# A residual stream kept by tokens instead of by features in a two-layer transformer trunk

## The chip, the cores and the metric

The kernel runs on one core of one Trainium2 chip. The metric is the device time of one execution in microseconds (us), the median of several runs. A profile of one execution stands beside it, with the busy time of each engine: PE (TensorE, the matrix products), PEld (the loading of the standing operand into TensorE, which overlaps PE), DVE (VectorE), ACT (ScalarE), POOL (GpSimd) and SP (SyncE, which here only issues DMAs).

## What is computed

The reference is a trunk of two macaron layers on 512 tokens of 1024 features, in float32:

```python
D_MODEL, SEQ, DEPTH, D_FF, NORM_EPS = 1024, 512, 2, 2816, 1e-6

def rms_norm(x, gain):
    inv = lax.rsqrt(jnp.mean(x * x, axis=-1, keepdims=True) + NORM_EPS)
    return x * inv * gain

def swiglu(h, w_gate, w_up, w_down):
    return (jax.nn.silu(h @ w_gate) * (h @ w_up)) @ w_down

for l in range(DEPTH):
    x = x + 0.5 * swiglu(rms_norm(x, ffn1_norm[l]), ffn1_wg[l], ffn1_wu[l], ffn1_wd[l])
    z = rms_norm(x, mix_norm[l]) @ w_in[l]            # q | k | v | conv_B | conv_C | conv_h
    attn = sliding_window_attention(q, k, v, sink[l])  # window 128, 8 heads of 64, 2 for k and v
    conv = B * depthwise_causal_conv3(C * h)
    x = x + concat([attn, conv]) @ w_out[l]
    x = x + 0.5 * swiglu(rms_norm(x, ffn2_norm[l]), ffn2_wg[l], ffn2_wu[l], ffn2_wd[l])
return rms_norm(x, final_norm)
```

The root in a norm is a sum over the 1024 features of one token, so it is one number for each token. The gain is one number for each feature.

## The kernel before

**Numbers as pairs.** Every operand of a product is cut into a rounded high part and a low part that holds the rest. Each product is then three: high by high, high by low, low by high, summed in PSUM. A weight tile (128 partitions x 1024 numbers, 512 KB) is loaded by SP, its high part is cast on ACT (`split`, L200), and DVE subtracts to get the low part (L201). In the "far" form (`split_far`, L203 to L207) ACT writes the negated raw tile as the low part, casts the high part after it, and a DMA that POOL issues adds the raw tile onto the low part; DVE isn't used.

**Fewer products.** Large products are done in a scheme with seven block products in place of eight (`CHAINS`, `FORMS`, `SHARES`). The activations are cut into four blocks, two halves of the features by two halves of the tokens (called b11, b21, b12, b22 and their sums t1 to t4, made by `Seven.make`), and the weights too (a11, a12, a22 and their sums s1 to s4). One step takes one of the operands with one form of the weights, and the accumulators x, w and y are read after each step. The sums of weight blocks are partly made by DVE in the raw tiles themselves: `need_split` adds s1 into the raw a11 tile in place (L222) when it comes to the form s2.

**One order for the weights.** `plan` (L320) writes down, before anything runs, the order in which weight tiles are needed. `take_split` hands out the next pair and asks for the split of the tile two places ahead (`SPLIT_AHEAD`), and `need_raw` asks for loads four units further ahead (`LOAD_AHEAD`). There are eight raw buffers and three each of the high and the low part. Each engine takes its instructions in the order of the program, so what is issued first goes first on that engine, whether or not PE needs it first.

**Layout.** Before, the residual x lies by features: `xs[c]` holds 128 features on the partitions and 512 tokens along the row. A product into x therefore has the weight standing in TensorE and the activations moving past it. In a full plain product 512 tokens move past (`group` L269, `level`, `down` L292 to L318). In a seven step that goes into x it is `stand` (L733, product at L740): half of the tokens at a time, rows of 256. The other form, `stream` (L749, product at L755), has the activations standing, 128 tokens at a time, and 512 columns of weights moving past; it gives its result by tokens. It serves the gate and up products of the fast blocks, whose results are then turned by TensorE transposes (L961), and the last FFN.

**Stages of one FFN.** An FFN is a list of stages: `p` is a plain block of 256 hidden features, `w` two such blocks in seven steps with `stream` (`winograd2`), `u` one block in seven steps with standing weights and rows of 256 (`winograd`), `d` the plain product into x for the blocks named, and `s` the product into x for four blocks in seven steps (`share`, L764). Three of the four FFNs use `INNER` or `LAST` (p of block 0, d of block 0, five `w`, two `s`, d of blocks 9 and 10), the first uses `FIRST`. The mix has its own body (`mix`, L1194) and ends with a share into x.

**Norms.** `Norm` (L406) works by features. As soon as a stretch of x is final, `take` or `take_half` multiplies it by the gain and splits it; no root is in it yet. Squares are summed over the feature tiles, and a product with a matrix of ones (`factors`) gives the sum over the partitions, hence `inv`, one number for each token in every partition. The first products of the next stage (block 0 of an FFN; k, v and the first q in a mix) run on the unscaled x, and their results are multiplied by `inv` on the way out of PSUM. `scale` then makes the fully scaled activations for the seven steps of the later blocks. In the mixes all projections run on unscaled x, and DVE and POOL multiply by `inv` afterwards. At the end `Finale` turns x to tokens by 32 transposes, in the first steps of a `w` stage.

The function that holds all this is `trunk_kernel`; the main loop is at L1405.

Of the kernel before, what the change touches and what calls it, by code (L numbers as in the profile page):

```python
# [39 lines left out]
LAST = INNER[:-1] + (("d", (9, 10)),)  # L40
# [16 lines left out]
)  # L57


@with_exitstack  # L60
def trunk_kernel(
# [49 lines left out]
    def form(name, dt=F32R, shape=(P, KC // 2, H)):  # L111
        return xpool.tile(list(shape), dt, tag="xf", bufs=14, name=name)
# [19 lines left out]
    NROW = 16 + 2 * 16 + 24  # L132
    rows = [work.tile([n, P], F32, tag=f"rows{n}", bufs=1, name=f"rows{n}") for n in (16, NROW - 16)]
    sink = const.tile([P, DEPTH * NH], F32, name="sink")

    def load_rest():
        for i, w in enumerate((mix_norm, ffn2_norm)):
            nc.sync.dma_start(
                rows[1][16 * i : 16 * i + 16, :], w.rearrange("l (c p) -> (l c) p", p=P)
            )  # L140
        nc.sync.dma_start(rows[1][32:56, :], conv_w.rearrange("l k (c p) -> (l k c) p", p=P))
        nc.sync.dma_start(sink, attn_sink.rearrange("l h -> (l h)").partition_broadcast(P))
# [10 lines left out]
    def turn_rows(i):  # L153
        n = rows[i].shape[0]
        rp = psum("aux", [P, n], f"par_ps{i}")
        nc.tensor.transpose(rp, rows[i], ident[:n, :n])
        nc.scalar.copy(par[:, 16 * i : 16 * i + n], rp)

    def gain_of(i, c):

        at = 16 * (i % 3) + 8 * (i // 3) + c
        return par[:, at : at + 1]

    def conv_of(l, k, c):
        at = 48 + 12 * l + 4 * k + c
        return par[:, at : at + 1]
# [121 lines left out]
    def abreast(kc):  # L288

        return max(1, KC // kc) if kc in (2, 4) else 1  # L290

    def level(n, hi, lo, rhs, wide):  # L292

        accs = [psum("mm", [P, S], f"acc_{n}_{j}") for j in range(wide)]
        cols = [slice(j * P, (j + 1) * P) for j in range(wide)]
        for k, (xh, xl) in enumerate(rhs):
            for j in range(wide):
                nc.tensor.matmul(accs[j], hi[:, k, cols[j]], xh, start=k == 0, stop=False)
                nc.tensor.matmul(accs[j], lo[:, k, cols[j]], xh, start=False, stop=False)
            for j in range(wide):  # L300
                nc.tensor.matmul(
                    accs[j], hi[:, k, cols[j]], xl, start=False, stop=k + 1 == len(rhs)
                )
        return accs

    def down(rhs, fresh=False):

        wide = abreast(len(rhs))
        for c in range(0, KC, wide):
            n, hi, lo = take_split()  # L310
            if fresh and c == 0:
                yield from enumerate(level(n, hi, lo, rhs, wide))
                continue
            for j in range(wide):
                cols = slice(j * P, (j + 1) * P)
                own = (f"{n}_{j}", hi[:, :, cols], lo[:, :, cols])
                tag = ("sc", "sc", "aux", "aux")[j] if fresh else "mm"
                yield c + j, group(rhs, own=own, tag=tag)  # L318

    def plan():  # L320
        def cols(src, k0, kc, n, how=None):
            wide = abreast(kc)
            for b in range(0, n, wide):
                order.append((add_unit((src, k0, kc, b * P, wide * P)), how))

# [15 lines left out]
        def seven(at, how):  # L341
# [6 lines left out]
            order.extend((u, (what, h, how(what, h))) for what in FORMS for h in range(2))  # L348

        def ffn(wg, wu, wd, stages):  # L350
            for what, b in stages:
                how = "far" if b == (0,) and stages is not FIRST else None
# [16 lines left out]
                if stages is not LAST or b[-1] < FF // (2 * P) - 1:  # L369
                    cols(wd, 2 * b[0], 2 * len(b), KC, how)  # L370
                    continue
                for half in range(2):
                    for k in range(0, 2 * len(b), 2):
                        u = add_unit((wd, 2 * b[0] + k, 2, half * S, S))
                        if half == 0:
# [18 lines left out]
    xpair = [xpool.tile([P, 2, S], F32, tag=f"x{c}", name=f"x{c}") for c in range(KC // 2)]  # L394
    xs = [xpair[c // 2][:, c % 2, :] for c in range(KC)]
# [10 lines left out]
    class Norm:  # L406
        def __init__(self, i):
            self.i = i
            self.h = [None] * KC
            self.acc = None  # L410
            self.inv = None
            self.pairs = {}
            self.begun = set()
            self.order = range(KC)

        def take(self, c, src=None):

            xc = xs[c] if src is None else src
            g = gain_of(self.i, c)
            if c % 2 == 0:  # L420
                self.pair = [form(f"x{n}_{self.i}_{c}", shape=(P, 2, S)) for n in "hl"]
            hi, lo = (t[:, c % 2, :] for t in self.pair)
            self.h[c] = (hi, lo)
            nc.scalar.activation(hi, xc, AF.Copy, scale=g)
            nc.vector.scalar_tensor_tensor(lo, xc, g, f32(hi), op0=ALU.mult, op1=ALU.subtract)

        def square(self, c):
            if self.acc is None:
                self.acc = work.tile([P, S], F32, tag="nacc", bufs=1, name=f"nacc_{self.i}")
                nc.scalar.activation(self.acc, xs[c], AF.Square)  # L430
                return
            sq = work.tile([P, S], F32, tag="nsq", bufs=2, name=f"nsq_{self.i}_{c}")
            nc.scalar.activation(sq, xs[c], AF.Square)
            nc.vector.tensor_add(self.acc, self.acc, sq)

        def take_half(self, o, t):


            self.order = (4, 5, 6, 7, 0, 1, 2, 3)
            at = slice(t * H, (t + 1) * H)  # L440
            for m in range(2 * o, 2 * o + 2):
                if m not in self.pairs:
                    self.pairs[m] = [form(f"x{n}_{self.i}_{m}", shape=(P, 2, S)) for n in "hl"]
                for j in range(2):
                    c = 2 * m + j
                    g = gain_of(self.i, c)
                    hi, lo = (p[:, j, at] for p in self.pairs[m])
                    self.h[c] = tuple(p[:, j, :] for p in self.pairs[m])
                    nc.scalar.activation(hi, xs[c][:, at], AF.Copy, scale=g)
                    nc.vector.scalar_tensor_tensor(  # L450
# [993 lines left out]
```

## Time and profile before

| | us |
|---|---|
| median of 3 runs | 1683.12 |
| lowest, highest run | 1682.5, 1683.18 |
| span of the profiled execution | 1681.6 |
| first product of PE after the start of the span | 1.19 |

The span reaches from the first to the last instruction that the profiler saw in one execution; the time of a run has a little more around it, 1.5 us between this span and the median. The page of the profile has numbered parts: busy time by engine; the span in 40 slices, each digit a busy share in tenths, with the clock that TensorE was granted; DMA queues; the chain of work that ended last; and the costliest groups of instructions. In such a group the line of the program comes first, then engine, operation, result <- operands, partitions x elements and the count; behind the bar stand the busy time, the mean of one in ns, and the idle time ahead of it with what ended it. Matmuls are pipelined, so the duration of one is longer than the distance to the next.

### The profile page before, as it was taken

The page shows a single profiled execution, that of the slowest core. Times are in us where ns is not written, and L with a number is a line of the kernel's source. Part 1 is how long each engine was busy: PE and PEld are TensorE (multiplying, and loading weights), DVE is VectorE, ACT ScalarE, POOL GpSimd, SP SyncE. Part 2 cuts the span into 40 slices and gives each one's busy share as a digit, 9 for nine tenths or more (in the row PEclk, how much of TensorE's full clock was granted, in tenths as well). Part 3 has the DMA queues.
Part 4 walks back from the last instruction along what each step waited for, and adds up shares of the span by engine and source line. Part 5 has one row for each costly group of instructions (what it writes and reads, how often), then busy time and mean ns, then how long its engine had stood idle before and what let it go on. Part 6 is the DMA issues. An engine that isn't in the chain of part 4 may idle for free.

```text
span 1681.6 us, 23537 instructions
## 1 busy us (share of the span) xinstructions
PE 1672.6 (99%) x9010; PEld 1444.0 (86%) x9010; DVE 1381.3 (82%) x1820; ACT 964.9 (57%) x1335; POOL 206.3 (12%) x185
## 2 busy tenths in 40 slices
PE   9999999999999999999999999999999999999998
PEld 7888889988898888889988888999888988888886
DVE  7987679988899877799798777997688997667995
ACT  6445565466566655564465555654565766555654
POOL 0011111001211111111011111110012111111111
PEclk9999999999999999999999999999999999999999
DMA  8467777731497777788567777784125867777881
GB/s 251 99 177 190 186 198 184 189 94 51 119 233 163 183 181 187 187 197 203 164 138 181 191 185 183 189 230 143 51 63 140 225 138 201 187 178 185 226 211 51
DMA packets 191590, 283.14 MB, mean 168 GB/s; under 512 B 9004, under 2 KB 77684, under 8 KB 191476
## 3 DMA queue, kind: packets, MB, share of 16 engines
q1 hardware_dynamic: 151572, 200.73, 37.8%
q0 software_dynamic: 39184, 80.23, 28.0%
q8 instruction: 71, 1.16, 0.3%
q10 hardware_dynamic: 720, 0.66, 0.1%
q14 instruction: 43, 0.35, 0.1%
HBM read 261.14 MB, written 2.10 MB: 157 GB/s over the span
## 4 chain that ended last, share of the span: by engine, by line
PE 97%; DVE 2%; DMA 0%; issue 0%; ACT 0%; SPq 0%; DVEq 0%; ACTq 0%
PE x L755 25%; PE y L755 12%; PE x_s L740 8%; PE acc L279 8%; PE acc L280 8%; PE acc L282 7%; PE w L755 6%; PE y_s L740 4%; PE x_s L755 3%; PE w_s L740 2%; PE at L961 2%; PE x_m L740 1%; PE y_m L740 1%; PE y_s L755 1%; PE acc L635 1%; PE pt L1291 1%
## 5 line engine op out<-in xcount | busy, mean ns | idle before, releaser
L200 ACT CAST wh<-raw 128x1024 fp32r<-128x1024 f32 (+1 forms) x486 | 507.5, 1045 | 546.5 <-PE x L755 129.1
L201 DVE TENSOR_TENSOR wl<-raw,wh 128x1024 fp32r<-128x1024 f32 (+1 forms) x486 | 589.2, 1215 | 203.6 <-ACT wh L200 202.2
L279 PE MATMUL acc<-xh,wh 128*128 128x512 f32 x424 | 166.5, 393 | 0.0
L280 PE MATMUL acc<-xl,wh 128*128 128x512 f32 x424 | 165.6, 391 | 0.0
L282 PE MATMUL acc<-xh,wl 128*128 128x512 f32 x416 | 162.3, 390 | 0.0
L195 POOL DMA_DIRECT2D raw<-in_ffn_wu_dram x39 | 48.9, 1254 | 416.9 <-DMA raw<-in_ffn_wu_dram 338.1
L280 PEld LDWEIGHTS acc<-xl,wh 128*128 128x128 f32 x424 | 79.7, 188 | 16.3 <-DVE xl L450 0.6
L279 PEld LDWEIGHTS acc<-xh,wh 128*128 128x128 f32 x424 | 79.8, 188 | 15.7
L282 PEld LDWEIGHTS acc<-xh,wl 128*128 128x128 f32 x416 | 78.1, 188 | 16.3
L195 POOL DMA_DIRECT2D raw<-in_ffn_wg_dram x39 | 47.6, 1243 | 223.6 <-DMA raw<-in_ffn_wu_dram 89.2
L227 DVE TENSOR_TENSOR raw<-raw,raw 128x1024 f32<-128x1024 f32 x58 | 70.3, 1219 | 3.8 <-DMA raw<-in_ffn_wu_dram 2.1
L195 POOL DMA_DIRECT2D raw<-in_ffn_wd_dram x32 | 38.6, 1205 | 260.6 <-DMA raw<-in_ffn_wd_dram 159.1
L755 PE MATMUL w<-wh,fb21h 128*128 128x512 f32 x152 | 60.7, 399 | 0.0
L755 PE MATMUL x<-wh,ft2h 128*128 128x512 f32 x152 | 60.6, 398 | 0.0
L755 PE MATMUL y<-wh,ft3h 128*128 128x512 f32 x152 | 60.4, 398 | 0.0
L755 PE MATMUL w<-wl,fb21h 128*128 128x512 f32 x152 | 59.4, 391 | 0.0
L755 PE MATMUL x<-wl,ft2h 128*128 128x512 f32 x152 | 59.3, 390 | 0.0
L755 PE MATMUL y<-wh,ft3l 128*128 128x512 f32 x152 | 59.2, 390 | 0.0
L755 PE MATMUL y<-wl,ft3h 128*128 128x512 f32 x152 | 59.2, 390 | 0.0
L755 PE MATMUL w<-wh,fb21l 128*128 128x512 f32 x152 | 59.2, 389 | 0.0
L755 PE MATMUL x<-wl,fb11h 128*128 128x512 f32 x152 | 59.2, 389 | 0.0
L755 PE MATMUL x<-wl,ft1h 128*128 128x512 f32 x152 | 59.2, 389 | 0.0
(504 smaller groups left out, 4814.6 us busy)
## 6 DMA issues: line engine op xcount, KB each, us to landing
raw<-in_ffn_wu_dram SPq DMA_DIRECT2D x126, 512.0 KB, 4.4
raw<-in_ffn_wd_dram SPq DMA_DIRECT2D x104, 512.0 KB, 5.0
raw<-in_ffn_wg_dram SPq DMA_DIRECT2D x86, 512.0 KB, 4.7
raw<-in_ffn_wu_dram POOLq DMA_DIRECT2D x39, 512.0 KB, 8.1
raw<-in_ffn_wg_dram POOLq DMA_DIRECT2D x39, 512.0 KB, 6.1
raw<-in_w_in_dram SPq DMA_DIRECT2D x36, 512.0 KB, 3.7
raw<-in_ffn_wd_dram POOLq DMA_DIRECT2D x32, 512.0 KB, 8.6
raw<-raw POOLq DMA_DIRECT2D x20, 512.0 KB, 6.8
```

The costliest lines, as they stand in the source:

```text
L195: nc.gpsimd.dma_start(out=r, in_=rows_of(*more), accum_op=ALU.add)
L200: nc.scalar.copy(hi, raw)
L201: eng.tensor_sub(lo, raw, f32(hi))
L227: nc.vector.tensor_add(a11, a11, s1)
L279: nc.tensor.matmul(acc, hi[:, k, :], rhs[k][0], start=k == first, stop=False)
L280: nc.tensor.matmul(acc, hi[:, k, :], rhs[k][1], start=False, stop=False)
L282: nc.tensor.matmul(acc, lo[:, k, :], rhs[k][0], start=False, stop=k == last)
L635: nc.tensor.matmul(opening[n], (lo if part == "w" else hi)[:, k, :], xl if part == "x" else xh, start=n not in begun, stop=k == KC - 1 and ...
L740: nc.tensor.matmul(accs[c // 2][:, c % 2, :], w[:, k, cols], x_[:, 2 * h + k, :], start=start and c % 2 == 0 and h + k + i == 0, stop=h + ...
L755: nc.tensor.matmul(accs[u], x_[:, 2 * h + k, tok], w[:, k, :], start=start and h + k + i == 0, stop=h + k == 2 and i == 2, skip_group_chec ...
L961: nc.tensor.transpose(tp[:, t * P : (t + 1) * P], ups[t][:, c * P : (c + 1) * P], ident)
L1291: nc.tensor.transpose(tp[:, h, :], self.p[:, h, kb * P : (kb + 1) * P], ident)
```

## The change

x is kept by tokens through the whole program: `xt(t, o)` is a tile of 128 tokens by 512 features, four token tiles and two feature halves, in the same memory as before.

- Every product into x now has the activations standing and 512 columns of weights moving past them. `stand` and `level` are gone; `share` always uses `stream`, and `down` works on four token accumulators for each half of the features.
- `Norm` is new. As each tile of x becomes final, ACT squares it and sums along the row. When the four tiles of a token half are there, `stage` makes the root of two token tiles on ACT and four small DVE operations, and `turn` multiplies each tile by the root and by the gain (loaded by `begin` as a row spread over all partitions, two DMAs of 256 KB on SP), transposes it in four 128 x 128 pieces on TensorE, and copies the result by ACT into the activations of the next stage. For a mix it is split into high and low parts by ACT and DVE instead. So the first products of the next stage take x already scaled.
- The order of the last three steps of a share is changed (`CHAINS2`, `SHARES`), so that the first token half is final after step 4 and the second after steps 5 and 6 (`ENDS`).
- `INNER` and `LAST` begin with `w` of block 0 and end the hidden blocks with `u` of block 10; block 8 joins the plain product at the end. The far form of the first weight moves with it, from block 1 to block 0.
- A mix opens k, v and the first q together, by token halves, with rows of 256; the multiplications by `inv` are gone.
- The first norm of the program keeps the old way, in a class `First`. `Finale` no longer needs its 32 transposes.

```diff
 INNER = (
-    ("p", 0), ("d", (0,)), ("w", 1), ("w", 3), ("w", 5), ("w", 7), ("w", 9), ("s", 1), ("s", 5),
-    ("d", (9, 10)),
+    ("w", 0), ("w", 2), ("w", 4), ("w", 6), ("w", 8), ("u", 10), ("s", 0), ("s", 4),
+    ("d", (8, 9, 10)),
 )
...
-SHARES = ((0, 0, 1), (0, 0, 1), (1, 0, -1), (1, 1, 1), (1, 1, -1), (1, 0, 1), (0, 1, 1))
+SHARES = ((0, 0, 1), (0, 0, 1), (1, 0, -1), (1, 1, 1), (1, 0, 1), (1, 1, -1), (0, 1, 1))
+ENDS = {1: (0, 0), 4: (1, 0), 5: (1, 1), 6: (0, 1)}
...
+CHAINS2 = CHAINS[:4] + (CHAINS[5], CHAINS[4], CHAINS[6])
...
+    def down(acts, blocks):
+
+        for o in range(2):
+            accs = [psum("mm", [P, S], f"down_{state['group']}_{t}") for t in range(NT)]
+            for i, b in enumerate(blocks):
+                _, wh, wl = take_split()
+                ah, al = acts[b]
+                for t in range(NT):
+                    tok = slice(t * P, (t + 1) * P)
+                    for k in range(2):
+                        for n, (a, w) in enumerate(((ah, wh), (al, wh), (ah, wl))):
+                            nc.tensor.matmul(
+                                accs[t],
+                                a[:, k, tok],
+                                w[:, k, :],
...
+                    if i + 1 == len(blocks):
+                        yield t, o, accs[t]
...
-                        lambda what, h: "far" if (b, what, h) == (1, "a11", 0) else None,
+                        lambda what, h: "far" if (b, what, h) == (0, "a11", 0) else None,
...
+        def begin(self):
+
+            self.gain = [g2(f"gain_{self.i}_{o}") for o in range(2)]
+            for o in range(2):
+                nc.sync.dma_start(
+                    self.gain[o], self.row[o * S : (o + 1) * S].partition_broadcast(P)
                 )
...
+        def __call__(self, t, o):
+
+            nc.scalar.activation(
+                junk(f"sq_{self.i}_{t}_{o}"),
+                xt(t, o),
+                AF.Square,
+                accum_out=self.ss[:, o * NT + t : o * NT + t + 1],
+            )
+            half = t // 2
+            self.seen[half] += 1
+            if self.seen[half] == 4:
+                self.stage(half)
+
+        def stage(self, half):
+
+            i = self.i
+            if half == 0:
+                self.rooms()
+            v, r, y = (small(f"{n}_{i}_{half}", 2) for n in "vry")
+            at = 2 * half
+            nc.vector.tensor_add(v, self.ss[:, at : at + 2], self.ss[:, NT + at : NT + at + 2])
+            nc.scalar.activation(r, v, AF.Abs_reciprocal_sqrt, scale=1.0 / D, bias=eps)
+            nc.vector.tensor_scalar(v, v, 1.0 / D, EPS, op0=ALU.mult, op1=ALU.add)
+            newton(y, r, v)
+            for o in range(2):
+                for t in (at, at + 1):
+                    self.turn(t, o, y[:, t - at : t - at + 1])
+                if half == 0 and not self.mixing:
+                    self.make(("b11", "b21")[o])
+            if half and not self.mixing:
+                self.make("t2")
+
+        def turn(self, t, o, by):
+
+            name = f"{self.i}_{t}_{o}"
+            tok = slice(t * P, (t + 1) * P)
+            xn = g2(f"xn_{name}")
+            nc.vector.scalar_tensor_tensor(
+                xn, xt(t, o), by, self.gain[o], op0=ALU.mult, op1=ALU.mult
+            )
+            tp = psum(self.tags.pop(0), [P, KC // 2, P], f"xt_{name}")
+            for j in range(KC // 2):
+                nc.tensor.transpose(tp[:, j, :], xn[:, j * P : (j + 1) * P], ident)
+            if self.mixing:
+                hi, lo = (p[:, :, tok] for p in self.parts[o])
+                nc.scalar.copy(hi, tp)
+                nc.vector.tensor_sub(lo, tp, f32(hi))
+            else:
+                nc.scalar.copy(self.full[o][:, :, tok], tp)
...
-        for step, (acc, operand, start) in enumerate(CHAINS):
+        for step, (acc, operand, start) in enumerate(CHAINS2):
...
-                if y is None:
-                    stand(accs[acc], wh, wl, xh, xl, h, start)
-                else:
-                    stream(accs[acc], wh, wl, xh, xl, h, start)
+                stream(accs[acc], wh, wl, xh, xl, h, start)
...
-                    if y is None:
-                        part = xpair[2 * o + m][:, :, t * H : (t + 1) * H]
-                    else:
-                        part = y[2 * t + m][o]
+                    part = xt(2 * t + m, o)
                     nc.vector.scalar_tensor_tensor(
                         part, accs[acc][m], by * sign, part, op0=ALU.mult, op1=ALU.add
                     )
+                    if after and step in ENDS:
+                        after(2 * t + m, o)
...
-        kacc, vacc, qacc = norm.groups(3)
...
+        held = [take_split(SPLIT_AHEAD - j) for j in range(3)]
+        kacc, vacc, qacc = opened = [psum("mm", [P, S], f"acc_{n}") for n, _, _ in held]
+        for t in range(2):
+            tok = slice(t * H, (t + 1) * H)
+            for j, (_, hi, lo) in enumerate(held):
+                for k in range(KC):
+                    xh, xl = (z[:, tok] for z in norm.h[k])
...
-        share(ops, 1.0, after.step, soon={(0, 1): ("t2",), (1, 0): ("t1",), (1, 1): ("t3", "t4")})
+        after.begin()
+        share(ops, 1.0, soon={(0, 1): ("t2",), (1, 0): ("t1",), (1, 1): ("t3", "t4")}, after=after)
```

More of the change, by code (lines that the diff above doesn't have):

```diff
@@ L286, in group @@
         return acc
[L288 to L318, printed above, removed]
+    def down(acts, blocks):
[12 more added lines that the diff above has]
+                                w[:, k, :],
+                                start=i + k + n == 0,
+                                stop=i + 1 == len(blocks) and k == 1 and n == 2,
+                            )
+                    if i + 1 == len(blocks):
+                        yield t, o, accs[t]
@@ L347, in seven @@
                     add_unit(*(at(o, j, h) for o, j in what))
-            order.extend((u, (what, h, how(what, h))) for what in FORMS for h in range(2))
+            order.extend((u, (what, h, how(what, h))) for what in forms for h in range(2))
         def ffn(wg, wu, wd, stages):
             for what, b in stages:
-                how = "far" if b == (0,) and stages is not FIRST else None
                 if what == "p":
@@ L526, in make @@
                     continue
-                hi, lo = (form(f"f{what}{n}_{self.name}") for n in "hl")
+                hi, lo = both(f"f{what}_{self.name}")
                 self.forms[what] = (hi, lo)
@@ L553, in room_form @@
     def room_form(name):
-        return [form(f"sum{n}_{name}", F32) for n in range(2)]
-    norm = Norm(0)
+        return both(f"sums_{name}", F32)
+    norm = First()
     s8 = small("s8", 2 * NT)
@@ L950, in winograd2 @@
                 turns(step)
-                if not first and step < 3:
-                    norm.make(CHAINS[step + 4][1])
+                if not first and step < 4:
+                    norm.make(("t3", "t1", "t4", "b22")[step])
                 if between:
```

386 lines of the change are left out of this document (145 added, 241 removed).

## Prediction

> **What bounds the kernel now.** I read the page first (busy shares, clock row, chain of work that ended last), then the list of who waited for whom on PE, then the merged chain in order of time for the pace of each kind of product.
>
> ```profile
> span 1681.6 us, 23537 instructions
> ...
> PE 1672.6 (99%) x9010; PEld 1444.0 (86%) x9010; DVE 1381.3 (82%) x1820; ACT 964.9 (57%) x1335; POOL 206.3 (12%) x185
> ...
> PEclk9999999999999999999999999999999999999999
> ...
> PE 97%; DVE 2%; DMA 0%; issue 0%; ACT 0%; SPq 0%; DVEq 0%; ACTq 0%
> ```
>
> ```profile
> PE idle L127 <- DVE warm L582: 1.2, 1, 1.2
> PE y_m L740 <- DVE wl L201: 0.5, 2, 0.3
> PE xt L601 <- DMA xin<-in_x_dram: 0.2, 1, 0.2
> ```
>
> PE is the bound from one end to the other: it stands still for 1.9 us in all, 97% of the chain is PE, and the clock is full after the first slice. DVE at 82% is next. So the time follows PE's own work plus whatever makes PE wait; any wait that the change opens is paid in full, because nothing else is on the chain.
>
> PE's work must be counted by pace, not by the duration of one product, since products overlap:
>
> ```profile
> 150.26 10.88 PE x L755 x48
> ...
> 740.58 5.75 PE x_s L740 x48
> 746.34 5.76 PE w_s L740 x48
> ```
>
> ```profile
> 172.82 0.38 PE L961 MATMUL at<-ident,u 128*128 128x128 f32 x2
> 173.04 0.38 PE L961 MATMUL at<-ident,p 128*128 128x128 f32 x2
> 173.25 0.38 PE L961 MATMUL at<-ident,u 128*128 128x128 f32 x2
> 173.47 0.38 PE L961 MATMUL at<-ident,p 128*128 128x128 f32 x2
> 173.61 0.47 PE L755 MATMUL y<-wh,ft3h 128*128 128x512 f32 x1
> ```
>
> A 512 wide product takes 10.88/48 = 0.2267 us, a 256 wide one 5.76/48 = 0.120, a 128 wide transpose (173.25 - 172.82)/4 = 0.108. So two products of 256 cost 0.240 where one of 512 costs 0.227.
>
> **The change: PE's own work.** Counts are from the code and from the instruction order of the two built programs.
>
> - Eight shares (two each in the three fast FFNs that end in `x<-`, one each in the two mixes) go from `stand` to `stream`: 336 products of 256 (40.3 us) become 168 of 512 (38.1), 2.23 each, -17.9.
> - In three FFNs `p` of block 0 (96 of 512, 21.8 us) becomes `u` of block 10 (168 of 256, 20.2): -4.8. The plain down products stay at 144 per FFN.
> - Norm sums by the ones matrix: ten products of 512 go, -2.3.
> - The mixes open with 144 products of 256 by token halves for 72 of 512: 2 x 0.96, +1.9.
> - Transposes: five norms x 32 come, the 32 at the end go: 128 x 0.108, +13.8. The longer end (block 8 joins it, block 0's down goes): +0.1.
>
> Sum -9.2 us; in all 5512 + 2976 + 520 products (512, 256, 128 wide) become 6408 + 1092 + 648.
>
> **DVE, ACT, DMA.** The programs hold 1741 DVE instructions for 1820, 1248 on ACT for 1244, 409 SP transfers for 398 (ten broadcasts of gains, issued one stage ahead, are hidden behind that stage), POOL loses its ten multiplications by `inv`. Totals are no bound. A share at 38.1 instead of 40.3 us could be, as its DVE work is nearly as long. The last FFN already has such a share:
>
> ```profile
> 1566.00:1607.00 41.00, 41.00 (x183) 33.95 (x182) 40.79 (x44) 23.69 (x24) 6.58 (x6) 1.00 0.90 234
> ```
>
> There PE runs 183 products in 41 us without a gap while DVE is at 40.79 of 41. So 0 is the near row; the far end is 1 us for each of four first shares, +4. I take 0.
>
> **The change: what now waits.** Before, the first products of a stage take x unscaled, and `inv` comes in behind them; a norm is off PE's path. After, x must be squared, rooted, scaled, transposed, copied and split before the stage's first product. Half of the tokens is turned ahead, the second half must fit behind two operands' products. Rows for this chain:
>
> ```profile
> L201 DVE TENSOR_TENSOR wl<-raw,wh 128x1024 fp32r<-128x1024 f32 x479 | 585.0, 1224 | 198.1 <-ACT wh L200 196.7
> ...
> L791 DVE SCALAR_TENSOR_TENSOR x<-x_s,x 128x512 f32<-128x512 f32 x48 | 31.8, 684 | 0.8
> ...
> L1156 DVE SCALAR_TENSOR_TENSOR ytok<-ytok,y_end,gain 128x512 f32<-128x512 f32 x3 | 2.2, 746 | 0.0
> ...
> L402 DVE TENSOR_TENSOR y_end<-r_end 128x1 f32<-128x1 f32 x4 | 0.6, 160 | 0.4 <-ACT r_end L1121 0.3
> ```
>
> ```profile
> L200 ACT CAST wh<-raw 128x1024 fp32r<-128x1024 f32 x479 | 503.7, 1052 | 544.8 <-PE x L755 129.1 <-issue 89.8 <-PE y L755 84.3
> L965 ACT COPY raw_a<-at 128x512 f32<-128x512 f32 x64 | 35.8, 586 | 3.1 <-PE at L961 3.0
> ...
> L496 ACT ACT_TABLE_LOAD x5 | 6.4, 1283 | 0.1
> ...
> L1115 ACT ACTIVATE ysq<-ytok 128x512 f32<-128x512 f32 x5 | 3.1, 629 | 6.1 <-DVE ytok L1113 6.0
> ...
> L1115 ACT ACTIVATION_READ_ACCUMULATOR ysq<-ytok 128x1 f32 x7 | 1.3, 186 | 0.0
> ...
> L695 ACT ACTIVATE r<-v,eps 128x4 f32<-128x4 f32 x1 | 0.3, 298 | 0.0
> ```
>
> ```profile
> L207 POOL DMA_DIRECT2D wl<-raw x9: 856/896/896, 523.1 to 1363.8; - x9
> ...
> DMA to landing us min/median/max: 4.4/7.5/8.9
> ```
>
> I walk each engine's queue in the order of the built program. Back to back, DVE operations follow each other about 0.08 us sooner than their durations say.
>
> *Mix to FFN (twice).* Zero is where PE ends step 4 of `share`, the last into token half 0, second column half. ACT: weight cast to 1.1, two squares to 2.7, table load to 4.0, root to 4.3. DVE: x update and three small operations to 5.4, a weight's low part to 6.6, four scaled tiles at 7.3 to 9.3. PE: step 5 to 5.4, then step 6 with the first transposes in it (0.35 lost) to 13.0. ACT meanwhile copies and casts b11 to 10.3, b21 to 13.1. DVE ends b11's low part at 11.5, and now stands the new wait: next in its queue is the add into the raw weight (L222), and that weight is the source of the "far" copy whose ACT part ended at 7.1 and which lands 7.5 later, 14.65. Queued behind it are both last x updates, b21's low part and the second half's scaling; ACT's squares and through them the cast of the b21 weight wait for them. So: add 15.8, x 16.4, b21 low 17.6, weight low 18.7, x 19.3, weight low 20.5, then (add, root, three small, add) 23.4 and scaled tiles 24.2 to 26.2. PE's queue has b21's products first: weight cast ready 18.4, four products, low part 20.5, eight products to 22.35; the next b21 weight lies in the buffer just read, cast 22.4 to 23.45, four products; transposes as the tiles come; streaming from 26.75. From 12.97 that is 13.8 us with 18 products and 16 transposes in it (5.8): idle 7.9 + 0.35 = 8.3. With a landing of 4.4 it is 5.2, with 8.9 it is 9.7.
>
> *FFN to FFN (once).* Zero is the start of the last down unit, 5.44 us long; its last two quarters are the other token half, so the first half has only 2.7 us of cover. The far copy leaves at -3.3 and lands at 4.2; the add into its source stands ahead of the first x update of the unit. DVE: add 5.4, weight low 6.6, x 7.2 and 7.8, add 8.9; ACT: squares 9.0, table 10.3, root 10.6; scaled tiles 11.9 to 13.9; first transpose 11.95, so PE stands 6.5 us. Then, as above, b11, b21, second root, second tiles 20.4 to 22.4, and PE streams from 22.9: 17.4 us after 5.44, work in it 5.5, idle 11.9 (8.8 to 13.0 by the landing).
>
> *FFN to mix (once).* No far copy. Squares of three quarters 5.8, table 7.1, root 7.4, tiles from 8.7; second tiles 16.2 to 18.2; PE streams at 18.7: 13.3 us less 8.3 of work, idle 5.0. *First FFN's share to mix (once)*: same chain with steps 5 and 6 as cover, idle 2.3 (0.3 + 0.7 + 1.3 at three places).
>
> Idle together 2 x 8.3 + 11.9 + 5.0 + 2.3 = 35.8, from 26.5 to 39.7 by the landing alone. If the cover were whole, 0.
>
> **The clock.** A long pause may cost more than itself:
>
> ```profile
> 1.19 2.74 PE L127 MATMUL idle<-zero 128*128 128x512 bf16 x6 [1.19 <-DVE warm L582]
> ...
> 4.91 1.49 PE L601 MATMUL xt<-ident,xin 128*128 128x128 f32 x6
> ...
> 8.20 0.60 PE L601 MATMUL xt<-ident,xin 128*128 128x128 f32 x4
> ```
>
> The same transposes come 0.21 apart at 4.9 us and 0.11 apart at 8.2: PE starts at half pace and keeps it for about 5.0 us from its first product. [...] From the rows, a fall costs 0 to half of 5.0 us, 2.5, per pause: 0 to 7.5. I take 2.5: only the FFN to FFN pause (6.5) is longer than the 5.0 us that the start shows.
>
> **Sum**, against the profiled execution: 1681.6 - 9.2 + 35.8 + 2.5 = 1710.7; the median of the runs, 1683.12, lies 1.5 above the span: 1712.
>
> **Rivals.**
> 1. *The cover is whole, and the change is faster.* If the second half's chain, from the last product into x to its last split, ends within the 10.9 us of products on b11 and b21, and PE finds those first in its queue ready, only PE's own work is left: 1683.1 - 9.2 = 1674. It decides at 2.7 us of first-half cover after an FFN and at 10.9 us after a share. For it: ACT is idle 43% of the time. Against it: by the rows the first half alone takes 6.5 us too long, and the built order puts b21 ahead of b11 and its raw add ahead of the x updates.
> 2. *Part of the waits is hidden*: far copies land at 4.4 and half of the rest overlaps, about 13 us idle: 1681.6 - 9.2 + 13 + 1.5 = 1687, up to 1699 where only the landing is early.
> 3. *The clock falls in every pause*: 1712 + 5 = 1717; with late landings (39.7) 1721.
> 4. *DVE becomes the bound in the faster shares*: +4, 1716, by the row above not likely.
> 5. *The change doesn't do what it says* (512 wide products slower with x standing): the row at 150.26 is that very form, so no.
>
> **How the numbers follow.** Forecast with waits about as walked (1699 to 1717, rival 4 within it): 0.60. Rival 3: 0.13. Rival 2: 0.17, a quarter of it within 0.2%. Rival 1: 0.10. The range leaves out rival 1 and the low part of rival 2 at one end and the last of rival 3 at the other: 1690 to 1722. A difference of 0.2% (3.4 us) is about what a measurement of this kernel can tell from none. Faster 0.10, same 0.05, slower 0.85.
>
> **What would show it.** In the page after: PE busy under 99%, idle of about 36 us, nearly all of it at five places, ahead of the first products on b21 and the norm transposes, put down to DVE (scaled tiles, weight low parts) and ACT (casts); DVE waiting for the far copy at the raw add three times; products of 512 at 0.227, shares of 38.1 us. If PE's pauses are absent the walk is wrong; if they are there but the time is 5 us higher with products 0.45 apart behind them, it is the clock; if PE waits inside shares, it is DVE.

## The result, and the profile after

The changed kernel takes **1748.2 us** (median of 4 runs, 1744.71 to 1752.14), the kernel before 1683.14 beside it: a ratio of 1.0388, 95% interval 1.0373 to 1.0403. The forecast was 1712, with a range up to 1722. The sign was right, the size was not: 65 us slower instead of 29.

The page of the changed kernel, its busy times and the granted clock:

```profile
span 1747.0 us, 21808 instructions
...
PE 1691.9 (97%) x8150; PEld 1408.2 (81%) x8150; DVE 1334.4 (76%) x1741; ACT 966.9 (55%) x1379; POOL 194.6 (11%) x175
...
PEclk9999999999998999999989999999999999999999
```

PE's busy time went up by 19 us although its work went down. Products at half speed account for some 11.8 us of that (9.2 and 2.6 in the table below), and two slices of the clock fell; the rest of the rise was not split. Who waited for whom on PE, longest first (columns: total us, times, longest):

```profile
PE w L742 <- ACT wh L195: 10.8, 4, 5.6
PE x_s L742 <- ACT wh L195: 8.0, 6, 2.6
PE xt L512 <- DVE xn L507: 7.5, 3, 3.9
PE y_m L742 <- DVE x L771: 4.5, 2, 2.5
PE x_s L742 <- DVE x L771: 3.6, 6, 0.8
PE y_s L742 <- ACT wh L195: 2.7, 3, 0.9
PE w L742 <- ACT fb L195: 2.1, 1, 2.1
...
PE y_s L742 <- DVE x L771: 1.1, 4, 0.6
```

Rows with `xt`, `w` are at the norms, as forecast. Rows with `x_s`, `y_s`, `y_m` are inside the shares, where the forecast had nothing. In the kernel before, all waits of PE together were 1.9 us.

To place the loss, PE's **lost time** is counted from the trace: the distance from the start of each product to the start of the next, less the pace of its kind (0.2267, 0.120 or 0.108 us). It holds the pauses and the extra time of products at half speed. Before, it was 10.2 us in all; after, 84.9. Span less lost time is PE's own work, with about 8 us ahead of the first product and behind the start of the last, which are the same in both: 1671.4 us before and 1662.1 after, 9.3 less. Each column is one profiled execution. In us, with the extra time of products at half speed that no pause follows in brackets:

| place | forecast | after | old order | and late splits | and no far copy | and no root |
|---|---|---|---|---|---|---|
| first FFN to mix | 2.3 | 2.1 | 3.0 | 3.0 | 3.0 | 0.5 |
| mix to FFN, first | 8.3 | 10.7 (3.0) | 11.8 | 13.4 | 10.0 | 2.0 |
| FFN to FFN | 11.9 + 2.5 | 11.9 (3.2) | 11.6 | 11.7 | 7.3 | 2.3 |
| FFN to mix | 5.0 | 5.7 (1.3) | 5.7 | 5.8 | 5.8 | 0.3 |
| mix to FFN, second | 8.3 | 10.0 (1.6) | 12.5 | 14.2 | 9.6 | 2.3 |
| five norms together | 38.3 | 40.3 (9.2) | 44.5 | 47.9 | 35.7 | 7.2 |
| shares and last products | 0 | 36.4 (2.6) | 12.2 | 4.8 | 4.8 | 4.7 |
| start and all the rest | 10.2 | 8.2 | 8.4 | 7.9 | 8.9 | 8.7 |

The four columns at the right are experiments, each with one more edit than the one to its left. The norms came out within 2 us of the forecast, but by luck in part: the pauses were 4.7 us shorter than forecast (31.1 for 35.8) and the clock cost 6.7 more (9.2 for 2.5). The miss in the sum is one row: 36.4 us in the shares, where the forecast took 0.

### The profile page after: what moved, and what is told of

Its sections match the earlier page's. It is cut to its first block, busy times and chain, and to the rows that moved or that the text cites. A ratio compares the mean times of both kernels' runs of the same rounds, so it can differ in the third digit from the quotient of the medians.

```text
span 1747.0 us, 21808 instructions
## 1 busy us (share of the span) xinstructions
PE 1691.9 (97%) x8150; PEld 1408.2 (81%) x8150; DVE 1334.4 (76%) x1741; ACT 966.9 (55%) x1379; POOL 194.6 (11%) x175
## 5 line engine op out<-in xcount | busy, mean ns | idle before, releaser
L195 ACT CAST wh<-raw 128x1024 fp32r<-128x1024 f32 (+1 forms) x500 | 520.8, 1045 | 572.4 <-PE x L742 134.2
L742 PE MATMUL x<-wh,fb 128*128 128x512 f32 x608 | 188.7, 391 | 0.0
L742 PE MATMUL x<-wh,ft 128*128 128x512 f32 x608 | 188.6, 391 | 0.0
L742 PE MATMUL y<-wh,ft 128*128 128x512 f32 x608 | 188.2, 391 | 0.0
L742 PEld LDWEIGHTS x<-wh,fb 128*128 128x128 f32 x608 | 114.4, 188 | 23.5
L742 PEld LDWEIGHTS x<-wh,ft 128*128 128x128 f32 x608 | 113.1, 188 | 22.8
L742 PEld LDWEIGHTS y<-wh,ft 128*128 128x128 f32 x608 | 113.1, 188 | 22.7
L742 PE MATMUL x<-wl,fb 128*128 128x512 f32 x304 | 118.5, 390 | 0.0
L742 PE MATMUL x<-wl,ft 128*128 128x512 f32 x304 | 118.3, 389 | 0.0
L742 PE MATMUL y<-wl,ft 128*128 128x512 f32 x304 | 118.0, 389 | 0.0
L742 PE MATMUL w<-wh,fb 128*128 128x512 f32 x304 | 100.6, 415 | 13.3 <-ACT wh L195 10.8
```

The costliest lines, as they stand in the source:

```text
L195: nc.scalar.copy(hi, raw)
L742: nc.tensor.matmul(accs[u], x_[:, 2 * h + k, tok], w[:, k, :], start=start and h + k + i == 0, stop=h + k == 2 and i == 2, skip_group_chec ...
```

## The experiments

**The order of a share's steps.** The change moved a22 (t4) ahead of s1 (t1), so that the first token half is final earlier. The accumulators then run x, w, x, y, y, x, x: a step sums into an accumulator that DVE must first read for the step before. And a22 is needed one step earlier. The edit puts the old order back:

```diff
-SHARED = ("a11", "a12", "s2", "s3", "a22", "s1", "s4")
+SHARED = FORMS
-SHARES = ((0, 0, 1), (0, 0, 1), (1, 0, -1), (1, 1, 1), (1, 0, 1), (1, 1, -1), (0, 1, 1))
-ENDS = {1: (0, 0), 4: (1, 0), 5: (1, 1), 6: (0, 1)}
+SHARES = ((0, 0, 1), (0, 0, 1), (1, 0, -1), (1, 1, 1), (1, 1, -1), (1, 0, 1), (0, 1, 1))
+ENDS = {1: (0, 0), 4: (1, 1), 5: (1, 0), 6: (0, 1)}
-CHAINS2 = CHAINS[:4] + (CHAINS[5], CHAINS[4], CHAINS[6])
+CHAINS2 = CHAINS
```

> Order of the last steps of a share put back (x, w, x, y, x, y, x, so that no two neighbouring steps sum into the same accumulator, and the weight a22 is needed one step later); all else as changed. Theory (the new order makes the share stalls): of the 36.3 us that PE loses inside the shares and the last products, only the 1.1 to 1.5 us at the third step of the shares behind a u block stay, some 8 us in all, so 28 us go; the first token half is final one step later, which costs up to 5.4 us at three norms: 1720 to 1736 us. Rival (DVE is full in the faster shares, in any order): the stalls move but stay, 1743 to 1753 us.

Measured 1731.69 us (ratio 1.0285, 1.027 to 1.030), within the theory's range. The lost time in the shares fell from 36.4 to 12.2 us, and that at the norms rose by 4.2, less than the walk's bound of 5.4 at three places. The longest waits of PE that are left:

```profile
PE xt L512 <- DVE xn L507: 20.3, 5, 5.9
PE w L742 <- ACT fb L195: 6.9, 3, 2.5
PE y_s L742 <- ACT wh L195: 5.4, 6, 0.9
```

All waits for DVE's x update (L771), 9.2 us in the list above, are gone. Six waits of `y_s` stay: the third-step stalls.

**Two more raw buffers.** In the changed kernel, PE's longest stall in a share is at the fifth step of the first share of the second FFN. Its line on PE, and the two casts on ACT that it waits behind (start, duration, operation, and in brackets the idle time ahead with what ended it):

```profile
775.44 2.07 PE L742 MATMUL x_s<-wh,ft_s 128*128 128x512 f32 x4 [2.59 <-ACT wh L195]
```

```profile
769.87 1.05 ACT L195 CAST wh<-raw 128x1024 fp32r<-128x1024 f32 x1 [1.68 <-DMA raw<-in_ffn_wd_dram]
...
773.40 1.99 ACT L195 CAST wh<-raw 128x1024 fp32r<-128x1024 f32 x2 [1.52 <-DMA raw<-in_ffn_wd_dram]
```

Here a load is late: a22's two tiles are the last that a share loads. Ten raw buffers for eight are to take that away, paid for with three of the g2 buffers (work tiles of 128 x 512 numbers):

```diff
-        return wpool.tile(list(shape), dt, tag="raw", bufs=8, name=name)
+        return wpool.tile(list(shape), dt, tag="raw", bufs=10, name=name)
-        return work.tile(list(shape), dt, tag="g2", bufs=14, name=name)
+        return work.tile(list(shape), dt, tag="g2", bufs=11, name=name)
```

> Ten raw weight buffers for eight, paid for with eleven g2 buffers for fourteen; all else as changed. Theory (in the shares the load of a22 starts late because its buffer is still held, and ACT's cast waits for the landing): the 2.6 us stall at the fifth step of the first share of an FFN and its half pace go, 2 to 4 us in each of three FFNs: 1736 to 1743 us. Rival (the loads are only late as DVE is late): no change, 1745 to 1750 us; if the missing g2 buffers bind, slower.

Measured 1743.42 us (1.0356, 1.0338 to 1.0373), just above the 1743 that was expected. That stall went from 4.4 us with its half speed to 1.3, and the waits of `x_s` for casts (L195) fell from 8.0 to 4.5 us. The lost time in the shares fell from 36.4 to 32.3 us in all, as a new wait of 2.7 us for DVE's x update came in the last FFN. So late loads are some 4 us of the order's 24. The other 20 us were not split further; the 9.2 us of waits for L771 are among them.

**No far copy at the norms.**

```diff
-                        lambda what, h: "far" if (b, what, h) == (0, "a11", 0) else None,
+                        lambda what, h: None,
```

> The first weight of block 0 is split on ACT and DVE like all others, instead of through a DMA that adds onto the low part; all else as changed. Theory (the raw add of DVE waits for that DMA, 15.2 us in three places, and the scaled tiles and weight parts wait behind it): the three norms ahead of an FFN lose 3 to 5 us less each, with less time at half pace behind them, less 1.2 us each for the low part now on DVE: 1736 to 1742 us. Rival (other links of the chain are as late, and DVE's extra operation eats the rest): 1746 to 1751 us.

Measured 1742.33 us (1.0347, 1.0327 to 1.0368), just above the expected 1736 to 1742. The three norms ahead of an FFN lost 7.1, 7.4 and 6.4 us instead of 10.7, 11.9 and 10.0, 11.6 less together; the shares lost 4.1 more, for which no cause was sought. In the changed kernel the wait itself is seen in DVE's queue at the FFN to FFN norm:

```profile
853.05 1.23 DVE L196 TENSOR_TENSOR wl<-raw,wh 128x1024 fp32r<-128x1024 f32 x1 [0.43 <-ACT wh L195]
864.49 1.22 DVE L222 TENSOR_TENSOR raw<-raw,raw 128x1024 f32<-128x1024 f32 x1 [10.21 <-DMA wl<-raw]
865.63 1.22 DVE L196 TENSOR_TENSOR wl<-raw,wh 128x1024 fp32r<-128x1024 f32 x1
866.77 1.28 DVE L1006 SCALAR_TENSOR_TENSOR x<-down,x 128x512 f32<-128x512 f32 x2
```

The raw add stands 10.2 us for the copy, and the x updates of the last product stand behind it: the wait that the prediction named.

**Zeros in the pauses.** Twelve products of zeros go ahead of the first transposes of the second half at four norms:

```diff
+            if o == 0 and t == 2 and self.i > 1:
+                spin(12, tp.rearrange("p a b -> p (a b)"))
```

> Twelve products of zeros on TensorE ahead of the transposes of the second token half at three norms (both mix to FFN, the FFN to FFN) and the last FFN to mix; their results are overwritten. All else as changed. Theory (behind a pause the products run at half pace, 9.1 us lost so at four norms): where the zeros fall into the pause they cost nothing and keep the pace, 1739 to 1745 us. Rival (the half pace has nothing to do with the pause, or the zeros stand in the way of real products): 1748 to 1757 us.

Measured 1750.98 us (1.0401, 1.0386 to 1.0417). Half speed at the four norms fell from 9.2 us to 5.9, and pauses from 29.0 to 26.8, but the 48 zeros are 10.9 us of work. The time is in the rival's range, by its second condition, that the zeros stand in the way of real products: at each of the two mix to FFN norms, of the ten zeros in the trace eight ran 21 to 28 us ahead of the pause, inside the mix's share, and two at the pause (516.6 and 516.8 us at the first). From the changed kernel the run can't be told apart clearly, as the two intervals overlap. So this edit doesn't buy the clock back; zeros that run in the pause alone were not tried.

**What makes the third-step stalls.** With the old order, six stalls of 1.55 to 1.7 us stay, one in each share of three FFNs. DVE and ACT at one of them, in the run with the old order; PE stalls from 795.1 us on:

```profile
790.99 1.28 DVE L771 SCALAR_TENSOR_TENSOR x<-x_s,x 128x512 f32<-128x512 f32 x2
792.19 1.21 DVE L543 TENSOR_TENSOR raw_a<-raw_a 128x1024 f32<-128x1024 f32 x1
793.32 2.35 DVE L222 TENSOR_TENSOR raw<-raw,raw 128x1024 f32<-128x1024 f32 x2
```

```profile
793.49 1.06 ACT L195 CAST ft_s<-raw_a 128x1024 fp32r<-128x1024 f32 x1 [5.18 <-DVE raw_a L543]
794.62 3.15 ACT L195 CAST wh<-raw 128x1024 fp32r<-128x1024 f32 x3
```

ACT stands still for 5.2 us, because the cast of t1 is ahead of the weight casts in its queue and t1 isn't there. DVE has no gap from 786.4 us on; it is late. Four runs asked why, all with the old order in them. First, is it buffers that the operands of the next share lack?

```diff
-        t = xpool.tile(list(shape), dt, tag="xf", bufs=8, name=name)
+        t = xpool.tile(list(shape), dt, tag="xf", bufs=9, name=name)
-        return work.tile(list(shape), dt, tag="g2", bufs=14, name=name)
+        return work.tile(list(shape), dt, tag="g2", bufs=10, name=name)
```

> The old order of a share's steps, and nine activation buffers (xf) for eight, paid for with ten g2 buffers for fourteen. With the old order alone, 1731.7 us, six shares still stall 1.55 to 1.7 us at their third step. Theory (DVE is full: a share holds 27 DVE operations of 1024 columns at 1.13 us and 14 x updates at 0.6, 39.0 us for 38.1 us of products): one more buffer changes nothing, 1728 to 1735 us. Rival (blocks 8, 9 and 10 hold three of the eight buffers through the shares, so that the operands of the next share are made late): the six stalls get smaller or go, 1720 to 1727 us.

Measured 1733.7 us (1.0297, 1.0281 to 1.0312); all six stalls stayed. One more buffer isn't it. Second, is it DVE's sum of work?

```diff
-            return Seven([raws[b], raws[b + 2]], room_form, f"s_{whole}_{b}")
+            return Seven([raws[b], raws[b + 2]], room_form, f"s_{whole}_{b}", far=("t4", "b22"))
```

> The old order of a share's steps, and in the FFNs' shares the operands t4 and b22 are split through ACT and a DMA (as the mixes' shares do) instead of on DVE, 2.3 us less DVE work in a share. Theory (DVE is full): the six stalls of 1.55 to 1.7 us at the third steps go or shrink to under 0.5, 1720 to 1726 us. Rival (buffers held, or the built order of PE, which puts a product of the next step ahead of the low parts): they stay, 1728 to 1735 us.

Measured 1739.97 us (1.034, 1.0323 to 1.0357): slower, outside both expectations. The stall of the first shares stayed at 1.6 us and that of the second FFN's second share fell to 0.8, but new ones came at other steps, 19.6 us in the shares for 12.2. What the copies cost there was not told apart. Third, does DVE come late into the shares? The change turns and splits blocks 8 and 9 inside the u block just ahead of them; the kernel before turns its last two blocks in the second share.

```diff
-                turns(step)
+                if first:
+                    turns(step)
...
-                share(then, 0.5, after=after if final else None)
+                share(then, 0.5, None if first else lambda step: 2 <= step < 6 and flush(1, "aux"), after=after if final else None)
```

> The old order of a share's steps, and the four transposes and splits of blocks 8 and 9 moved out of the u block ahead of the shares into steps 2 to 5 of the second share, as the kernel before has them. Theory (DVE comes into the shares late, as the u block and these splits, 2.7 us, stand ahead of them): the third-step stall of the first share of each FFN falls from 1.55 to under 0.5, that of the second stays, 1726 to 1730 us. Rival (the place of t1 in DVE's queue makes the stall, however early DVE is): all six stay, 1729 to 1735 us.

Measured 1724.32 us (1.0244, 1.0228 to 1.0259), below both ranges. All six stalls went, those of the second shares too, where the theory had let them stay (0.8 us in small pieces is left there), and the shares lost 4.8 us. The longest waits of PE:

```profile
PE xt L512 <- DVE xn L507: 22.0, 5, 6.6
PE w L742 <- ACT fb L195: 6.8, 3, 2.3
```

Not one `x_s` or `y_s` is among the longest. DVE does the same work in all, and the second share now holds more of it, yet it fits if DVE doesn't start behind. As the edit touches nothing in the first share and both shares lost their stalls, a delay from the u block must have been carried through both. Fourth, the queue order by itself: t1, t4 and b22 made one step later.

```diff
-            if not soon and step < 3:
-                ops.make(CHAINS2[step + 4][1])
+            if not soon and 0 < step < 4:
+                ops.make(CHAINS2[step + 3][1])
```

> The old order of a share's steps, and t1, t4 and b22 of an FFN's share are made one step later each, so that DVE's subtraction for t1 and ACT's cast of it don't stand ahead of the sums and casts of the weights of the third step. Theory (what is late there is queue order: x update, t1, two weight sums, then three casts): all six stalls of 1.55 to 1.7 us shrink to under 0.7, 1721 to 1727 us. Rival (DVE's sum of work, 39.0 us for 38.1, is the bound): PE loses about 1 us per share elsewhere in it, 1727 to 1733 us.

Measured 1726.76 us (1.0257, 1.024 to 1.0274): the shares lost 5.8 us; three stalls went and three shrank to 0.8. So the stall takes both: DVE late, and t1 ahead of what is needed first. Either cure is nearly enough. The sum of DVE's work, the rival of this run and the theory of the first two, is not the bound.

**The edits together.** First with the copies of the second run above, t4 and b22 through ACT and a DMA:

> All that the runs so far point to: old order of a share's steps, t4 and b22 of the FFNs' shares split through ACT and a DMA, first weight of block 0 split like all others. Theory (the three act in different places, so their gains add: 16.5 and 6 us from the median of the changed kernel, and 9 to 13 from the norms): 1710 to 1720 us, still slower than before, as the norms' chains keep some 30 us of pauses. Rival (the gains overlap): 1722 to 1730 us.

Measured 1734.27 us (1.0303, 1.0287 to 1.0318), slower than both ranges. The norms lost 7.7 us less than with the old order alone, and the shares, with these copies, 12.9 more. Then with the late splits in their place:

> The version to which the runs point: old order of a share's steps, splits of blocks 8 and 9 late as in the kernel before, first weight of block 0 split like all others. Theory (the far copy costs 4 us at each of the three norms ahead of an FFN, as the run with that edit alone had it, and no stall in the shares comes back): 1724.3 less 12, 1710 to 1715 us, 27 to 32 us above the kernel before, all but some 10 of it in pauses at the five norms and the half speed behind them. Rival (with the old order the pauses are set by other links): 1718 to 1725 us.

Measured **1713.98 us** (1.0183, 1.0166 to 1.020), as the theory had it: 31 us above the kernel before, with 35.7 us of lost time at the norms and 4.8 in the shares. It is the fastest of the versions that leave nothing out, and it does not reach the kernel before.

**The norms without the root.** To see what sets the pauses that are left, the squares, their sum, the root and the small operations behind it are left out; x is scaled by the gain alone, so this run computes another function.

```diff
         def __call__(self, t, o):
 
-            nc.scalar.activation(
-                junk(f"sq_{self.i}_{t}_{o}"),
-                xt(t, o),
-                AF.Square,
-                accum_out=self.ss[:, o * NT + t : o * NT + t + 1],
-            )
...
-            nc.vector.tensor_add(v, self.ss[:, at : at + 2], self.ss[:, NT + at : NT + at + 2])
-            nc.scalar.activation(r, v, AF.Abs_reciprocal_sqrt, scale=1.0 / D, bias=eps)
-            nc.vector.tensor_scalar(v, v, 1.0 / D, EPS, op0=ALU.mult, op1=ALU.add)
-            newton(y, r, v)
...
-                xn, xt(t, o), by, self.gain[o], op0=ALU.mult, op1=ALU.mult
+                xn, xt(t, o), 1.0, self.gain[o], op0=ALU.mult, op1=ALU.mult
```

> As the version with the three edits, but the norms leave out squares, sum, root and the small operations behind it: x is scaled by the gain alone (so the function computed is another), and all else of the turn stays. Theory (the root's chain, 0.82 us of square, 0.16 of sum, 1.58 of table and root, 0.64 of small operations, 3.2 us, is on the path once in each of five norms and in part again for the second half): 16 to 25 us less than with it, 1687 to 1697 us. Rival (the scaled tiles, transposes, copies and splits set the pauses, and DVE's weight parts between them): under 10 us less, 1702 to 1710 us.

Measured 1684.13 us (1.0006, 0.9997 to 1.0016): 29.9 us less, more than the theory had. The page of this run:

```profile
span 1682.7 us, 21664 instructions
...
PE 1667.9 (99%) x8150; PEld 1397.6 (83%) x8150; DVE 1325.3 (79%) x1694; ACT 928.7 (55%) x1280; POOL 191.7 (11%) x172
```

```profile
PE w L731 <- ACT wh L195: 1.8, 2, 0.9
PE xt L501 <- DVE xn L496: 1.7, 2, 1.4
```

The five norms lose 7.2 us instead of 35.7. So scaling, transposing, copying and splitting do nearly fit behind the other token half; it is the chain ahead of them, from the squares over the root on ACT to the small operations on DVE, that doesn't. Which of its links weighs most was not split. And with this chain at no cost at all the version would stand where the kernel before stands, 1684 to 1683.

**Pauses made on purpose.** The kernel before, with a chain of small DVE operations in five blocks, which a product of zeros waits for:

```diff
+                if step == 4 and norm.i == 2:
+                    hold = work.tile([P, H], F32, tag="hold", bufs=1, name=f"hold_{b}")
+                    nc.vector.tensor_scalar(hold, accs["y"][1][:, :H], 0.0, 0.0, op0=ALU.mult, op1=ALU.mult)
+                    for _ in range({1: 16, 3: 22, 5: 28, 7: 36, 9: 46}[b]):
+                        nc.vector.tensor_scalar(hold, hold, 0.0, 0.0, op0=ALU.mult, op1=ALU.mult)
+                    none = hold.bitcast(BF16)
+                    for u in range(2):
+                        nc.tensor.matmul(
+                            accs["x"][u], none[:, :P], none, start=False, stop=False,
+                            skip_group_check=True,
+                        )
```

> The kernel before, with a chain of 17, 23, 29, 37 and 47 small DVE operations in five blocks of the second FFN, on which a product of zeros waits that is summed into an accumulator: five pauses of PE of growing length, from near 0 to some 6 us, with full work on both sides. Theory (a pause brings half speed once it is long enough): the shortest pauses have none behind them, those over 2.5 us have 3.4 us or a multiple of it, at a cost of about 1.6 us each. Rival (half speed in the changed kernel comes of something else, as its denser shares): none behind any of them.

One run, 1753.07 us. The chains also held up DVE's other work, so the pauses came in groups. Blocks one, two, three and four: the stretch, its length, the busy time of PE, PEld, DVE, ACT and POOL (with the number of instructions), the granted clock, the busy share of the DMA engines and GB/s:

```profile
560.00:582.00 22.00, 18.68 (x76) 13.19 (x75) 19.39 (x33) 8.25 (x9) 2.41 (x2) 1.00 0.93 257
600.00:634.00 34.00, 27.55 (x106) 19.99 (x106) 19.12 (x37) 11.52 (x14) 3.61 (x3) 0.90 0.66 159
652.00:687.00 35.00, 26.59 (x107) 19.35 (x106) 21.31 (x43) 11.52 (x14) 3.61 (x3) 0.90 0.65 156
705.00:744.00 39.00, 27.72 (x108) 20.27 (x107) 24.01 (x51) 11.52 (x14) 3.61 (x3) 0.87 0.59 145
```

Block one, with three pauses of 0.8 to 1.1 us and two shorter ones between stretches of products, kept the clock. Block two, 2.0 and 0.9 us with only transposes around them, lost it for 6.83 us; block three (2.0 and 2.8) for 6.83, block four (2.0 and 5.9) for 10.24, block five (16.5) for 17.07, most of it inside the pause. In products the loss was about 2.4, 1.0, 2.4 and 1.6 us: it doesn't grow with the pause. So the rival fell, as half speed came with the pauses alone; the theory was right but for its limit of 2.5 us, since the longest pause of block two was 2.0.

## Why the prediction was right in sign and wrong in size

- *PE's own work, -9.2.* Right: span less lost time fell by 9.3.
- *The pauses at the norms, 35.8.* Right in place and nearly in size. The five cost 31.1 us without the half speed. The walk was long at the FFN to FFN norm (11.9 for 8.7), and its mechanism, the far copy at the raw add, was shown by the run without it, 11.6 us at three norms. What the walk took as one chain, from the squares to the small operations, is the greater part of what was left: 28.5 us at the norms by the run without it.
- *The clock, +2.5.* Too small: products at half speed cost 9.2 us at the norms and 2.6 in the shares. The upper bound of 2.5 for one pause fell too, as two of them cost 3.0 and 3.2. That a pause brings half pace at all, and in how many places, was the author's estimate: the trace of the kernel before has half pace only at its start, for about 5.0 us from the first product, and no run shows a term of 2.5 for one pause of 6.5. In its place the runs showed stretches of 3.41 to 13.65 us at half speed behind pauses of 2.7 to 5.7 us. The rival with a fall in every long pause was nearer on this term (7.5 us); it alone would have given 1717 to 1721.
- *The shares, 0.* This is the step that failed. "So 0 is the near row; the far end is 1 us for each of four first shares, +4. I take 0." Measured: 36.4 us with the last products. The row that it rests on was true of a share with the old order of steps, in which DVE kept up. The change has another order and a u block with its splits just ahead, and neither was priced: the prediction uses the new order only for when a token half ends. In place of 0 the runs showed 24.1 us for the order and 7.4 us for DVE coming behind from the u block; 4.8 us stay. Of the 24.1, 9.2 are waits for an accumulator that DVE has not read yet and some 4 come of a22 loaded too late; the cause of the rest is open. A DVE that is 99% busy without making PE wait was not a sign of safety: the delay which it brought along stayed through two shares.
- *The range.* Its upper end, 1722, was built of late landings and the clock alone. The rival "DVE becomes the bound" looked at the right place, but it was priced, at +4, by the sum of DVE's work; what DVE cost, 7.4 us, came of when it begins, and for the order of the steps there was no rival at all. So the sign that the prediction gave, "if PE waits inside shares, it is DVE", would have led astray: 24 of the 36 us went with the order.

## What to carry to other kernels

When a change permutes the steps of a scheme with few accumulators, write the sequence of accumulators out: a step that sums into the one that was just finished waits for the read of it (9.2 us of waits here), and a weight that is needed earlier needs its buffer earlier (some 4 us here). An engine that is nearly full beside the bound can carry a delay from one stage through the next, as DVE did here (7.4 us in the shares), so ask what it has in its queue when the stage begins, not only how much work the stage holds. A normalisation that is moved ahead of the products that it scales puts the whole chain of its root on the path: here that was 30 us, more than the 9 us of product time that the new layout saves.

## What the runs showed of the hardware

**Half speed behind pauses.** In the clock record of the changed kernel's profile the granted clock is 0.5 six times between the first microseconds and the end of PE's work: from 498.81 us on for 3.41 us, from 522.71 for 10.24, from 775.29 for 3.41, from 870.87 for 13.65, from 1222.44 for 3.41 and from 1396.52 for 6.83. Each of the six begins inside a pause of PE or at most 1.4 us behind its end; the pauses, counted like the lost time above, are of 2.7, 3.9, 2.8, 4.1, 3.5 and 5.7 us. At half speed, products of 512 follow each other at 0.43 us (498.99 to 499.85), from 502.56 on, at full speed, at 0.227. The longest pause of this profile that had none behind it is one of 2.1 us, ended at 1373.14. In the run with pauses made on purpose, pauses of 2.0 and 0.9 us in one block were enough for 6.83 us of half speed, and three of 0.8 to 1.1 in another brought none. So the length of one pause doesn't settle it alone; what does was not shown.
